# Attention stage: low halves of the weights by an adding DMA onto minus the high halves

## Chip, cores and metric

One core of a Trainium2 chip runs the whole kernel. The metric is the device time of one execution, in microseconds (us). All times are from runs on the chip.

## What is computed

A two-layer backbone over 512 latent tokens and 256 context tokens, model width 1024, everything in float32:

```python
for i in range(2):
    x = macaron_ffn(x, ...)                       # SwiGLU, width 2816
    xn = modulate(x, ...)                         # RMSNorm, scale and shift
    y = attn_mixer(xn, xn_ctx, ...) if i == 0 else conv_mixer(xn, ...)
    x = x + m[5] * y
    x = macaron_ffn(x, ...)
return rmsnorm(x, final_g)
```

The mixer of layer 0 is what matters here. One input projection gives queries, keys and values for 8 neighbourhood heads (an 8 x 16 window with a relative bias, plus all context keys) and for 4 differential heads (two softmax maps of each, the second subtracted with a factor lambda, then an RMSNorm). Their outputs are concatenated and go through one output projection.

## The kernel before

**Products.** TensorE multiplies in float32r, which keeps fewer bits than float32, so every operand is held as two float32r tiles, `hi` (rounded) and `lo` (what the rounding left). A float32 product is three of TensorE's: hi x hi, hi x lo and lo x hi (`mm3`, L134 to L140).

**Weights.** `load_w` (L109 to L116) brings one weight tile of 128x1024 float32 (512 KB) from HBM into a `raw` buffer by a DMA of SyncE's queue. ScalarE copies it to `hi`, which rounds (L114). Then one engine subtracts, `lo = raw - hi` (L115). `raw`, `wh` (hi) and `wl` (lo) have three buffers each, so a buffer comes free when the weight three before it has been used.

```python
nc.scalar.activation(hi[:, :n], raw[:, :n], AF.Copy)
(eng or wl_eng[0]).tensor_tensor(lo[:, :n], raw[:, :n], hi[:, :n], op=ALU.subtract)
```

**Who subtracts.** `wl_eng[0]` is VectorE for most of the kernel. For the attention stage it is set to GpSimd, because VectorE has the softmax there, and set back to VectorE after it. It is set after the first step of the projections, so that GpSimd subtracts for 23 weights: 13 of the query and key projections, 6 halves of value projections and 4 of the differential half of the output projection.

**Order of the stage.** Two generators run side by side. `projections()` emits the projections weight by weight. `attention()` emits, unit after unit, the scores, the softmax and the products with the values. A loop advances the projections by the time that the attention's products take on TensorE, so that TensorE has a projection to do while ScalarE and VectorE work at a softmax. A scheduler then puts each engine's instructions in an order of its own; every engine runs its own list strictly in that order.

Names that the prediction uses:
- L694: products of a value projection, L140 all others. L761 and L763: scores. L873 and L997: transposes of the weights of the softmax (`P`) before the products with the values, L888 and L973. L897: a product with ones, for the norm of a differential head; it waits for a square that ScalarE makes (L895).
- VectorE in the softmax of the differential heads: L846 the maximum, L853 to L855 small vectors, L856 to L858 scaling `P` and adding the second map. L248: a step of the head's norm. L754: the lo half of a key. L958: scaling `P` in the neighbourhood heads. L943 adds the bias.
- ScalarE: L848, L850, L851, L950 exponentials; L121 the hi half of what comes out of a product.
- GpSimd: L115 the 23 subtractions; L712 a product of the rotary embedding; L908 fills the bias tiles.

Of the kernel before, what the change touches and what calls it, by code (L numbers as in the profile page):

```python
# [10 lines left out]
F32R = mybir.dt.float32r  # L11
AF = mybir.ActivationFunctionType
ALU = mybir.AluOpType
# [5 lines left out]
KD = D // P            # chunks of the model width  # L19
N = 512                # latent tokens  # L20
NC = 256               # context tokens
# [7 lines left out]
BLOCKS = [(0, 4), (4, 4), (8, 4), (12, 6), (18, 4)]   # (first f chunk, chunks)  # L29
BLOCKS0 = [(0, 6), (6, 6), (12, 6), (18, 4)]                  # layer 0, first FFN  # L30
# [11 lines left out]
def build(tc, A, out):  # L42
    """A: name -> DRAM AP (host layouts, see kernel()); out: [128, 8, 512] feature-major."""
# [4 lines left out]
    with ExitStack() as es:  # L48
# [9 lines left out]
        def uid(s):  # L58
# [4 lines left out]
        BUFS = {"xn": 16, "h": 12, "P": 4,                                                 # 3 KB per partition  # L63
                "x": 12, "sc": 2, "pj": 6, "pv": 4, "P1": 4, "aux": 4,                     # 2 KB
                "nh": 7}                                                                   # 1 KB
# [7 lines left out]
        def tmp(n):  # L73
            """temporary of a norm"""
            if n > 256:
                return dt_("pj")
            return dp.tile([P, 256], F32, tag="nh", bufs=BUFS["nh"], name=uid("nh"))

# [16 lines left out]
        wl_eng = [nc.vector]  # L95

        def load_wx(src, tiles, lo):
            """in halves of 512 columns; tiles: two for each part"""
# [10 lines left out]
        def load_w(src, n=1024, eng=None):  # L109
            raw = wp.tile([P, 1024], F32, tag="raw", bufs=3, name=uid("raw"))  # L110
            nc.sync.dma_start(raw[:, :n], src)
            hi = wp.tile([P, 1024], F32R, tag="wh", bufs=3, name=uid("wh"))
            lo = wp.tile([P, 1024], F32R, tag="wl", bufs=3, name=uid("wl"))
            nc.scalar.activation(hi[:, :n], raw[:, :n], AF.Copy)  # L114
            (eng or wl_eng[0]).tensor_tensor(lo[:, :n], raw[:, :n], hi[:, :n], op=ALU.subtract)  # L115
            return hi, lo  # L116

        def split(hi, lo, src, scale=None):
            """hi + lo == src * scale exactly (scale a power of two)"""
# [9 lines left out]
        def after_mm(i):  # L129
            """not scheduled before the last matrix product emitted so far"""  # L130
# [4 lines left out]
        def mm3(outs, w, x, segs, first, last):  # L135
            """outs[i] += w^T x[:, segs[i]] with the three products that float32 needs"""
# [17 lines left out]
        wx = [dt_("x", dtype=F32R) for _ in range(4)]           # for weights of the start  # L154
# [4 lines left out]
        def load_c(nm):  # L159
            """silu of the vector on every partition"""  # L160
# [31 lines left out]
        def mod_step(l, m, ch, dve, pool=(), paced=True, early=False):  # L192
            """the streams in dve are summed on the vector engine, those in pool on GpSimd and ScalarE"""
# [38 lines left out]
        def mod_scale(l, m, i, s="c", out=None, ks=slice(0, KD)):  # L232
            """norm_g * (1 + scale)"""
# [6 lines left out]
        def rsqrt(ps, n, width):  # L240
            """(ps / width + eps) ** -0.5, with one Newton step after the table"""
# [10 lines left out]
        class Norm:  # L252
            """sum of squares gathered chunk by chunk (two partial sums), then 1/rms on every partition"""
# [5 lines left out]
            def add(self, xk, pre=False):  # L259
                """pre: have the table of rsqrt loaded by the time the sum is there"""  # L260
                n, i = self.n, min(self.k // 4, 1)
                if self.k >= self.parts:            # summed on the tensor engine
# [19 lines left out]
        def modulate_chunk(k, xk, y, s, b, hi, lo):  # L282
# [3 lines left out]
            if n <= 256 and k % 3 == 2:             # a part of them on ScalarE and GpSimd  # L286
# [12 lines left out]
        class Entry:  # L299
            """the input of a sub-layer: modulated norm of x, one token segment at a time"""  # L300
# [26 lines left out]
        class Head:  # L327
            """first products of a sub-layer, k outermost and one token segment at a time,
            so that they run while the rest of the input is still being made"""

            def __init__(self, units):
                # units: [(weight source, {segment: PSUM})], the PSUM allocated when used
# [3 lines left out]
            def run(self, e, si, ks=range(KD), inner=False):  # L336
                """inner: k innermost, so that the weights are freed one after the other"""
# [9 lines left out]
        def transition(e, down, head):  # L347
            """down(si): last products of the sub-layer before, segment si (calls e.norms[si].add);
            head(): makes the Head; statistics and products of neighbouring segments overlap"""
# [26 lines left out]
        def last_proj(e, srcs, nk, hl, evict):  # L376
            """output projection with nk chunks of input: the last three weight units are kept and used
            one token segment at a time"""
# [27 lines left out]
        class FFN:  # L406
# [6 lines left out]
            def head(self):  # L413
                """gate and up of chunk 0, gate of chunk 1"""
# [42 lines left out]
            def after_head(self, e):  # L457
                """finish chunk 1 (its up product); returns with chunks 0 and 1 done for the latents"""
# [31 lines left out]
            def body(self, e, first=2):  # L490
                """everything up to the last block's gate and up"""
# [10 lines left out]
            def tail(self, e2):  # L502
                """down products of the last block, one segment at a time"""
# [4 lines left out]
                held = {}                       # the three units loaded last  # L508
# [36 lines left out]
        # ================= layer 0: FFN 0 =================  # L545
        # the latents' part of the first chunks starts as soon as its modulation is there
# [83 lines left out]
        # ================= layer 0: attention =================  # L630
# [13 lines left out]
        # the residual waits in DRAM  # L644
# [4 lines left out]
        # differential lambda on every partition  # L649
# [22 lines left out]
        def proj_fm(src, outs):  # L672
            """outs: (segment, what takes the result) one after the other"""
# [9 lines left out]
        def proj_v(src, res, stack):  # L683
            """256 columns of a value projection, token-major, 3 tiles of 128 tokens per buffer: hi and lo in
            buffers of their own, or (stack) for each head of width 64 side by side, the second head lo first"""
# [30 lines left out]
        # Two heads (or maps) of width 64 share a chunk. For each, the moving operand stacks the  # L716
        # hi and lo parts of k over the 128 rows of the array and the stationary one holds hi of q
        # twice, so that one product gives qh kh + qh kl; ql kh is a second one on 64 rows.
# [3 lines left out]
        def q_parts(q, src, dst, scale):  # L722
            """src: 128 rows; dst: column view to write"""
# [32 lines left out]
        def scores(key, parts):  # L756
            """for (out, m, qs, ks) in parts: out = q k^T of head or map m, query columns qs, key columns given by
            the view ks; the products on 64 rows come together (outs in different banks)"""
# [64 lines left out]
        class Diff:  # L823
            """two query tiles of one differential head"""
# [77 lines left out]
        # neighbourhood heads: token order t' = column * 8 + row; query tiles are  # L902
# [359 lines left out]
```

## Time and profile before

| | |
|---|---|
| time, median of 3 runs | 2302.9 us |
| lowest, highest | 2297.8, 2303.41 us |
| span of the profiled execution | 2304.0 us |
| TensorE busy in that span | 2224.3 us, 97% |
| VectorE busy | 1372.8 us, 60% |
| ScalarE busy | 869.8 us, 38% |
| GpSimd busy | 284.1 us, 12% |
| mean granted TensorE clock | 0.989 |

The span runs from the first to the last instruction of one profiled execution; nothing else of that execution has a time of its own, and its span is 1.1 us over the median of the timed runs. A busy share is an average over stages. The stage that the change touches lies at about 655 to 985 us of the span.

### The profile page before, as it was taken

The numbers are of one execution on the slowest core, as the hardware profiler recorded it, in microseconds if no ns is written. First come the engines' busy times: TensorE is split into PE (matmuls) and PEld (weight loads), VectorE is DVE, ScalarE is ACT, GpSimd is POOL, SyncE is SP. The second block draws the span as 40 slices with busy tenths as digits, with TensorE's granted clock in tenths as the row PEclk, the third lists the DMA queues.
The fourth block names the chain that finished last, engine by engine and source line by source line (L and its number), as shares of the span: only waits on it lengthen the run. The fifth ranks groups of instructions, "written<-read, shape, count | busy, mean of one in ns | idle before, by whom it ended". The sixth has DMA issues, their size and how long they took to land.

```text
span 2304.0 us, 30465 instructions
## 1 busy us (share of the span) xinstructions
PE 2224.3 (97%) x11728; PEld 1889.3 (82%) x11728; DVE 1372.8 (60%) x2388; ACT 869.8 (38%) x1489; POOL 284.1 (12%) x196
## 2 busy tenths in 40 slices
PE   5899999999989999999999999999999999999998
PEld 3688888888878788788888888888889889888887
DVE  8893763534788876775555467555437446434335
ACT  4651421212456766652222244222225224222224
POOL 4550520000232311120000010000001001000001
PEclk9999999999999999999999999999999999999999
DMA  7672443434520111315555454444332322333232
GB/s 243 220 230 90 140 133 105 149 103 128 160 69 29 48 39 53 101 48 165 172 169 165 143 163 156 156 159 152 109 107 95 100 93 92 93 100 96 87 109 74
DMA packets 109993, 279.07 MB, mean 121 GB/s; under 512 B 14100, under 2 KB 18452, under 8 KB 109848
## 3 DMA queue, kind: packets, MB, share of 16 engines
q1 hardware_dynamic: 109848, 277.13, 38.5%
q8 instruction: 91, 1.49, 0.3%
q14 instruction: 54, 0.44, 0.1%
HBM read 272.88 MB, written 4.19 MB: 120 GB/s over the span
## 4 chain that ended last, share of the span: by engine, by line
PE 84%; DVE 10%; ACT 3%; issue 2%; POOL 1%; DMA 1%; SPq 0%; DVEq 0%; ACTq 0%; POOLq 0%
PE S L140 39%; PE acc L140 38%; PE acc L694 3%; DVE junk L210 1%; DVE wl L115 1%; PE S L763 1%; DVE xn L292 1%; PE acc L973 1%; DVE sm L215 1%; PE S L761 1%; PE acc L997 1%; DVE nh L285 1%; ACT wh L114 0%; POOL P L205 0%; PE acc L888 0%
## 5 line engine op out<-in xcount | busy, mean ns | idle before, releaser
L140 PE MATMUL S<-xn,wh 128*128 128x512 f32 (+1 forms) x3008 | 924.8, 380 | 20.8 <-ACT xn L291 12.5
L114 ACT ACTIVATE wh<-raw 128x1024 fp32r<-128x1024 f32 (+1 forms) x354 | 364.5, 1031 | 1072.2 <-PE acc L140 516.5
L140 PEld LDWEIGHTS S<-xn,wh 128*128 128x128 f32 x3008 | 555.9, 189 | 135.6 <-ACT xn L291 15.5
L115 DVE TENSOR_TENSOR wl<-raw,wh 128x1024 fp32r<-128x1024 f32 (+1 forms) x331 | 398.8, 1206 | 430.9 <-ACT wh L114 428.1
L140 PE MATMUL S<-xn,wl 128*128 128x512 f32 (+1 forms) x1504 | 569.0, 378 | 6.3 <-DVE wl L115 6.3
L140 PE MATMUL acc<-h,wh 128*128 128x512 f32 (+1 forms) x2148 | 534.6, 347 | 2.9 <-DVE x L470 2.8
L140 PE MATMUL acc<-xn,wh 128*128 128x256 f32 (+1 forms) x1664 | 451.1, 332 | 3.7 <-ACT xn L291 1.6
L140 PEld LDWEIGHTS acc<-h,wh 128*128 128x128 f32 x2148 | 364.2, 190 | 59.4 <-ACT h L121 3.1
L140 PE MATMUL acc<-h,wl 128*128 128x512 f32 (+1 forms) x1074 | 345.0, 344 | 1.4 <-DVE wl L115 1.4
L140 PEld LDWEIGHTS S<-xn,wl 128*128 128x128 f32 x1504 | 285.0, 190 | 61.5 <-DVE wl L115 8.3
L140 PEld LDWEIGHTS acc<-xn,wh 128*128 128x128 f32 x1664 | 297.1, 193 | 32.1 <-issue 2.7
L140 PE MATMUL acc<-xn,wl 128*128 128x256 f32 (+1 forms) x832 | 273.1, 329 | 3.2 <-DVE wl L115 3.2
L470 DVE SCALAR_TENSOR_TENSOR x<-acc,sm,x 128x512 f32<-128x512 f32 (+1 forms) x216 | 132.2, 629 | 220.1 <-PE acc L140 219.8
L140 PEld LDWEIGHTS acc<-h,wl 128*128 128x128 f32 x1074 | 192.4, 189 | 26.4 <-DVE wl L115 1.8
L270 POOL TENSOR_TENSOR nh<-nh,nh 128x256 f32<-128x256 f32 x42 | 45.4, 1085 | 1233.2 <-ACT nh L266 898.8
L210 DVE SCALAR_TENSOR_TENSOR junk<-aux,sc 128x512 bf16<-128x512 f32 x256 | 192.6, 752 | 1.6
L140 PEld LDWEIGHTS acc<-xn,wl 128*128 128x128 f32 x832 | 159.3, 192 | 16.9 <-DVE wl L115 4.1
L205 POOL TENSOR_TENSOR P<-aux,pv 128x512 f32<-128x512 f32 x64 | 106.3, 1674 | 131.5 <-ACT P L208 67.5
L121 ACT ACTIVATE h<-P 128x512 fp32r<-128x512 f32 (+2 forms) x99 | 62.5, 631 | 109.9 <-DVE P L429 109.8
L122 DVE TENSOR_TENSOR h<-P,h 128x512 fp32r<-128x512 f32 (+2 forms) x99 | 76.2, 769 | 20.1 <-ACT h L121 20.1
L694 PE MATMUL acc<-wh,xn 128*128 128x256 f32 x384 | 79.4, 295 | 1.5 <-DVE h L122 1.5
L115 POOL TENSOR_TENSOR wl<-raw,wh 128x1024 fp32r<-128x1024 f32 x23 | 56.7, 2468 | 185.6 <-ACT wh L114 185.6
(177 smaller groups left out, 1760.1 us busy)
## 6 DMA issues: line engine op xcount, KB each, us to landing
aux<-modw SPq DMA_DIRECT2D x288, 256.0 KB
raw<-wu SPq DMA_DIRECT2D x92, 512.0 KB
raw<-wg SPq DMA_DIRECT2D x91, 512.0 KB
raw<-wd SPq DMA_DIRECT2D x59, 512.0 KB
raw<-wd SPq DMA_DIRECT2D x48, 384.0 KB
raw<-cin SPq DMA_DIRECT2D x24, 512.0 KB
h<-modw SPq DMA_DIRECT2D x32, 256.0 KB
raw<-win SPq DMA_DIRECT2D x16, 512.0 KB
```

The costliest lines, as they stand in the source:

```text
L114: nc.scalar.activation(hi[:, :n], raw[:, :n], AF.Copy)
L115: (eng or wl_eng[0]).tensor_tensor(lo[:, :n], raw[:, :n], hi[:, :n], op=ALU.subtract)
L121: nc.scalar.activation(hi, src, AF.Copy)
L122: nc.vector.tensor_tensor(lo, src, hi, op=ALU.subtract)
L140: last_mm[0] = nc.tensor.matmul(o, a, b[:, s0:s1], start=first and ti == 0, stop=last and ti == 2)
L205: nc.gpsimd.tensor_mul(pr, raw, sc[s][h])
L210: i = nc.vector.scalar_tensor_tensor(junk, raw, 1.0, sc[s][h], op0=ALU.mult, op1=ALU.mult, accum_out=a)
L215: nc.vector.scalar_tensor_tensor(o[:, ch:ch + 1], pt[:, 0:1], pt[:, 1:2], modb[:, c:c + 1], op0=ALU.add, op1=ALU.add)
L270: (nc.gpsimd, nc.vector)[i].tensor_add(self.ss[i][:, :n], self.ss[i][:, :n], sq[:, :n])
L285: nc.vector.scalar_tensor_tensor(t[:, :n], xk, s[:, k:k + 1], y, op0=ALU.mult, op1=ALU.mult)
L470: nc.vector.scalar_tensor_tensor(v, ps, g[:, d:d + 1], v, op0=ALU.mult, op1=ALU.add)
L694: last_mm[0] = nc.tensor.matmul(o, a, b, start=k == 0 and ti == 0, stop=k == KD - 1 and ti == 2)
```

## The change

In the attention stage `lo` is made in another way. ScalarE writes minus the rounded weight into `lo`, a DMA issued from GpSimd's queue adds `raw` to it in place, and ScalarE then copies `raw` to `hi`. There is no subtraction on an engine there any more. Elsewhere nothing changes. The rest of the diff deletes comments and docstrings.

```diff
@@ load_w
             hi = wp.tile([P, 1024], F32R, tag="wh", bufs=3, name=uid("wh"))
             lo = wp.tile([P, 1024], F32R, tag="wl", bufs=3, name=uid("wl"))
+            if wl_eng[0] is None:
+                nc.scalar.activation(lo[:, :n], raw[:, :n], AF.Copy, scale=-1.0)
+                nc.gpsimd.dma_start(lo[:, :n], raw[:, :n], accum_op=ALU.add)
+                nc.scalar.activation(hi[:, :n], raw[:, :n], AF.Copy)
+                return hi, lo
             nc.scalar.activation(hi[:, :n], raw[:, :n], AF.Copy)
             (eng or wl_eng[0]).tensor_tensor(lo[:, :n], raw[:, :n], hi[:, :n], op=ALU.subtract)
@@ build, at the start of the attention stage
         advance()
-        wl_eng[0] = nc.gpsimd
+        wl_eng[0] = None
```

Lines of the changed kernel from L114 on: the two ScalarE copies are L115 (`lo`) and L117 (`hi`), the adding DMA is L116, and every line behind them stands 5 further down.

GpSimd's list at the start of the stage, before (`wl`, `wh` and `raw` are buffers of one weight each, `x` is of the rotary embedding):

```order
L115 TENSOR_TENSOR wl_6282<-raw_6279,wh_6281 128x1024
L115 TENSOR_TENSOR wl_6395<-raw_6392,wh_6394 128x1024
L115 TENSOR_TENSOR wl_6480<-raw_6477,wh_6479 128x1024
L115 TENSOR_TENSOR wl_6640<-raw_6637,wh_6639 128x1024
L712 TENSOR_TENSOR x_6379<-x_6379,x_5997 128x512
L115 TENSOR_TENSOR wl_6646<-raw_6643,wh_6645 128x1024
```

The same place now:

```order
L116 DMA wl_6282<-raw_6279 128x1024
L116 DMA wl_6396<-raw_6393 128x1024
L116 DMA wl_6482<-raw_6479 128x1024
L116 DMA wl_6643<-raw_6640 128x1024
L717 TENSOR_TENSOR x_6380<-x_6380,x_5997 128x512
L116 DMA wl_6650<-raw_6647 128x1024
```

Each subtraction has become the issue of a DMA at the same place of the list; the rotary products stand behind them as before.

ScalarE's list a little later, around the softmax of a differential head, before (`P` is the softmax of a unit, `S` its scores, `pv` the hi half of a transposed `P`):

```order
L121 ACTIVATE pv_6984<-acc_6979 128x512
L850 ACTIVATE P_6953,sm_6951<-S_6956,sm_6951 128x512
L851 ACTIVATE P_6954,sm_6951<-S_6956,sm_6951 128x256
L121 ACTIVATE pv_7005<-acc_7000 128x512
L114 ACTIVATE wh_7311<-raw_7309 128x1024
L848 ACTIVATE P_7032,sm_7031<-S_7035,sm_7031 128x768
L708 ACTIVATE x_7053<-acc_6975 128x512
```

The same place now:

```order
L126 ACTIVATE pv_6990<-acc_6985 128x512
L855 ACTIVATE P_6958,sm_6956<-S_6961,sm_6956 128x512
L856 ACTIVATE P_6959,sm_6956<-S_6961,sm_6956 128x256
L126 ACTIVATE pv_7011<-acc_7006 128x512
L117 ACTIVATE wh_7219<-raw_7217 128x1024
L117 ACTIVATE wh_7319<-raw_7317 128x1024
L853 ACTIVATE P_7038,sm_7037<-S_7041,sm_7037 128x768
L713 ACTIVATE x_7059<-acc_6981 128x512
L126 ACTIVATE pv_7088<-acc_7083 128x512
L855 ACTIVATE P_7039,sm_7037<-S_7042,sm_7037 128x512
L856 ACTIVATE P_7040,sm_7037<-S_7042,sm_7037 128x256
L115 ACTIVATE wl_7320<-raw_7317 128x1024
```

Ahead of the first exponential of the next softmax (L848 before, L853 now) there stood one copy of a weight, and now there are two; the second of these weights gets its `lo` only behind that softmax.

## Rows read from the trace of the kernel before

**Rows 1.** The page: shares of the chain that ended last, by engine.

```profile
PE 84%; DVE 10%; ACT 3%; issue 2%; POOL 1%; DMA 1%; SPq 0%; DVEq 0%; ACTq 0%; POOLq 0%
```

**Rows 2.** Stretch table of the stage: engines' busy us, then granted clock, DMA share, GB/s.

```profile
655.00:985.00 330.00, 307.01 (x1861) 260.10 (x1860) 253.24 (x448) 215.13 (x441) 69.92 (x34) 0.97 0.18 54
```

**Rows 3.** Page's costliest groups: GpSimd's subtractions (busy, mean ns, idle before).

```profile
L115 POOL TENSOR_TENSOR wl<-raw,wh 128x1024 fp32r<-128x1024 f32 x23 | 56.7, 2468 | 185.6 <-ACT wh L114 185.6
```

**Rows 4.** VectorE's instructions by line in the stage: ns min/median/max, first and last start.

```profile
L857 DVE SCALAR_TENSOR_TENSOR P<-P,sm,P x16: 736/744/2833, 682.0 to 827.8; 128x512 f32<-128x512 f32 x16
...
L858 DVE SCALAR_TENSOR_TENSOR P<-P,sm,P x16: 474/483/2602, 682.7 to 830.5; 128x256 f32<-128x256 f32 x16
...
L958 DVE TENSOR_SCALAR P<-P,sm x16: 475/486/2522, 846.8 to 974.4; 128x512 f32<-128x512 f32 x16
...
L754 DVE TENSOR_TENSOR h<-x,h x8: 684/686/2783, 661.4 to 779.0; 64x512 fp32r<-64x512 f32 x8
...
L248 DVE TENSOR_TENSOR nh<-nh,nh x8: 414/422/2450, 710.4 to 857.8; 128x256 f32<-128x256 f32 x8
...
L853 DVE TENSOR_TENSOR sm<-sm x16: 145/158/2348, 679.9 to 826.7; 128x1 f32<-128x1 f32 x16
```

**Rows 5.** Timeline at 682 us: start, us, engine, instruction, [idle before it].

```profile
682.25 5.31 POOL L115 TENSOR_TENSOR wl<-raw,wh 128x1024 fp32r<-128x1024 f32 x2 [17.23 <-ACT wh L114]
...
682.70 2.60 DVE L858 SCALAR_TENSOR_TENSOR P<-P,sm,P 128x256 f32<-128x256 f32 x1
```

**Rows 6.** Chain that ended last, in the stage: start, us, what.

```profile
662.79 2.78 DVE h L754
...
682.78 2.52 DVE P L858
685.30 2.28 DVE sm L853
...
763.29 1.06 ACT wh L114
...
827.79 2.83 DVE P L857
...
859.06 1.06 ACT wh L114
...
938.25 2.52 DVE P L958
```

**Rows 7.** Timeline of TensorE: products before which it idled.

```profile
667.13 0.39 PE L694 MATMUL acc<-wh,xn 128*128 128x256 f32 x1 [1.46 <-DVE h L122]
...
728.18 0.70 PE L897 MATMUL acc<-nh,ones 128*128 128x256 f32 x2 [2.79 <-ACT nh L895]
...
772.37 0.70 PE L897 MATMUL acc<-nh,ones 128*128 128x256 f32 x2 [1.31 <-ACT nh L895]
...
941.26 0.55 PE L761 MATMUL S<-h,pj 128*128 128x256 f32 x1 [2.63 <-DVE S L943]
```

**Rows 8.** Stretch table: one of 20 us (columns as in rows 2).

```profile
680.00:700.00 20.00, 17.18 (x85) 13.26 (x85) 17.24 (x30) 10.71 (x22) 7.99 (x4) 0.91 0.19 56
```

**Rows 9.** ScalarE's copies of weights in the stage: ns min/median/max, first and last start.

```profile
L114 ACT ACTIVATE wh<-raw x26: 1053/1060/1075, 661.4 to 982.2; 128x1024 fp32r<-128x1024 f32 x26
```

**Rows 10.** Timeline: two weights' copies on ScalarE, their first hi x lo products on TensorE.

```profile
749.15 1.06 ACT L114 ACTIVATE wh<-raw 128x1024 fp32r<-128x1024 f32 x1 [1.11 <-PE acc L694]
...
763.74 0.39 PE L140 MATMUL acc<-xn,wl 128*128 128x512 f32 x1
...
908.69 1.06 ACT L114 ACTIVATE wh<-raw 128x1024 fp32r<-128x1024 f32 x1 [0.88 <-PE acc L694]
...
922.47 0.40 PE L140 MATMUL acc<-xn,wl 128*128 128x512 f32 x1
```

**Rows 11.** One weight load: its issue, and DMA busy tenths, 699 to 704 in 40 slices.

```profile
699.75 0.35 SPq L111 DMA_DIRECT2D raw<-win  x1
...
DMA  0000000000000996994368999897323021000000
```

## The prediction

> **What bounds the kernel now.** The chain of work that ended last says that TensorE is the bound: 84% of it, VectorE 10%, ScalarE 3% [rows 1]. So a change beside TensorE counts only where TensorE waits for it. The stretch table of the stage says how much that is: of 330 us TensorE is busy 307.0, so 23.0 us are idle, and the granted clock is 0.97, so part of it ran at 1.2 GHz in place of 2.4. VectorE is busy for 253.2 us, ScalarE for 215.1, GpSimd for 69.9 [rows 2]. The 23 subtractions make 56.7 us of GpSimd's time, and behind GpSimd nobody waits for them in that row or in the chain [rows 1, 3]. Read that far, the change looks like work moved off an idle engine.
>
> The groups by line say otherwise. The same VectorE instruction takes 0.48 us as a rule and up to 2.60 (L858), 0.16 and up to 2.35 (L853, one number per partition), 0.49 and up to 2.52 (L958) [rows 4]. The timeline shows why: the 2.60 us of L858 begin at 682.70, after GpSimd has begun two subtractions at 682.25 [rows 5]. A VectorE instruction that comes up during a subtraction ends only when the subtraction does, and a subtraction takes 2.47 us [rows 3]. And these are not idle instructions: nine stretched ones, of 2.28 to 2.83 us, stand in the chain of the stage, the first at 662.79, the last at 938.25 [rows 6].
>
> **What the removal of the subtractions gives.** The nine pieces (one each of L754, L853, L248 and L958, two of L857, three of L858) add up to 22.9 us. At their lines' medians [rows 4] they would take 0.69 + 3 x 0.48 + 0.16 + 0.42 + 2 x 0.74 + 0.49 = 4.7 us. The difference is 18.2 us.
>
> From below I bound it by TensorE's idle time. Six idle times stand behind stretched instructions, the first 1.46 us at 667.13, the last 2.63 at 941.26, 14.5 us in all. Two of them, as the 2.79 at 728.18, are before L897, where TensorE idles for 1.31 us without any subtraction too [rows 7], so 14.5 - 2 x 1.31 = 11.9 us are the subtractions' own. From above there is the clock. In the 20 us after one such wait it reads 0.91 [rows 8]: 0.09 x 20 = 1.8 us lost at the lower level. Over the whole stage the loss is 0.03 x 330 = 9.9 us [rows 2]; the one dip at the start of the stage, behind a wait for VectorE's own last subtractions, stays, so 8.1 may come back. Ends: 11.9 and 20.0 us. I take 18.2, the chain's own figure, which lies near the upper end because a shorter wait also spares the low clock.
>
> **What ScalarE pays.** 23 more copies at 1.06 us [rows 9], 24.4 us on an engine that is busy for 65% of the stage. In the chain three of the 23 copies appear, the first at 763.29, the last at 859.06, 1.06 us each [rows 6]: 3.2 us if each is followed by a second one. The order of the changed program does that at the first of them: two copies stand ahead of the next softmax's first exponential where one stood. With VectorE's stretches gone ScalarE is later relative to it, so I count as many again: 6.4 us. Ends: 3.2 and 24.4.
>
> **What the DMA costs.** Nothing, as long as it lands before the first product with `lo`. Nothing in this trace adds by DMA, so I bound it. A load of the same 512 KB was issued at 699.75; its bytes run from 700.6 to 702.9, 3.2 us after the issue [rows 11]: the lower end, 1.0 us to start and 2.3 of moving. For the upper end I let three passes of the bytes (read `raw`, read `lo`, write `lo`) follow one another, 6.9 us, put one whole load of 2.3 ahead of them, and give GpSimd as long for the issue as for a subtraction: 1.0 + 6.9 + 2.3 + 2.5 = 12.7 us. I take 8, in the middle, since DMA engines stand at a share of 0.18 in the stage [rows 2] and no load is likely to be ahead.
>
> The cover: the tightest weight's copy begins at 908.69 and ends 1.06 later, and its first product with `lo` begins at 922.47, 12.7 us later; the next one has 763.74 - 750.21 = 13.5 [rows 10]. The others have more. Eight fits; 12.7 just does. Where the `lo` copy has moved behind a softmax, as in the order of the change, part of the cover goes with it; for the two tightest weights the changed program makes `lo` first, so I count none of it lost. If the cover goes, TensorE waits for the rest of the DMA, weight by weight.
>
> **What else moves.** `raw` is now held until the DMA has landed and `hi` is made, a few us longer than before; the load that waits for it on SyncE's queue, and the bias tiles' loads behind that, are late by as much. Of the 330 us a weight takes 14 on average and three buffers are loaded ahead, so I cost it at nothing. On GpSimd the rotary products (L712) stand behind the issues instead of behind 2.5 us subtractions: nothing, or a gain. No weight product is added or removed.
>
> **Sum.** 2304.0 - 18.2 + 6.4 = 2292.2 us for the profiled execution; the median of the runs is 1.1 us under that span, so I forecast **2291 us**, 12 less. Ends of the terms: 2302.9 - 20.0 + 3.2 = 2286 and, with the low gain and half of ScalarE's upper end, 2302.9 - 11.9 + 12.2 = 2303. A measurement of this kernel tells a difference from 0.3% on, that is, outside 2296 to 2310.
>
> **Rivals.**
>
> *ScalarE takes the gain back.* If half of the new copies or more fall ahead of something that TensorE waits for, they cost 12.2 us and up. For it: ScalarE at 65% and in strict order, with softmax and evictions in one list. Against: three in 23 were on the chain. With the 18.2 gained, 2302.9 - 18.2 + 12.2 = 2297; with all 24.4, 2309. Its middle is 2302: no change.
>
> *The adding DMA is late: slower.* It decides from the point where the two tightest weights alone eat the gain: (L - 12.7) + (L - 13.5) = 11.8, so at L = 19 us from copy to landing; earlier, if others join. At L = 25 these two cost 12.3 + 11.5 = 23.8, which gives 2291 + 24 = **2315**, and more with each further weight. For it: three buffers, a DMA that reads two streams and writes one, and a queue that no instruction of this kernel has used for data. Against: even my upper end is 12.7. The Trainium skill, "DMA: Bandwidth & Descriptors", section "Anatomy of one DMA", fits a DMA from GpSimd's queue as 2.0 us + bytes / 436 GB/s, an estimate of 3.2 us for 512 KB, or 4.4 with the second stream counted as bytes; it is fitted to plain copies and no run here shows it. By it this rival would hardly have a chance; by the rows it keeps 0.15.
>
> *GpSimd still holds VectorE up.* The issue on GpSimd may stretch VectorE as a subtraction did; then the change does not do what it says. L958, which has one tile from SBUF and a scalar, was stretched just as those with two [rows 4]. If all issues hold as long as subtractions, nothing is gained and 6.4 lost: 2309. The Trainium skill, "SBUF — State Buffer", section "Who interferes with whom", has the second input of a two-input VectorE instruction shut out only by a GpSimd instruction that reads SBUF, and has descriptor writing need the write side alone. By that L857, L858, L853, L754 and L248 would run free and only L958's kind could be held, which would leave the sum at 2291 + 2 = 2293; the trace shows the blocking of both kinds, and no issue of this sort.
>
> **Chances.** Forecast 0.58, ScalarE's rival 0.18, late DMA 0.15, GpSimd's hold 0.09. Faster by over 0.3%: 0.58 and a little of the last, 0.60. Within 0.3%: most of ScalarE's rival and half of the last, 0.20. Slower: the late DMA and the far ends of the other two, 0.20. The range reaches from the best ends of both terms, 2286, less 6 of the 23.0 - 14.5 = 8.5 us that TensorE idles for other reasons and that a changed order of its products may spare, 2280, to just past the first price of the late DMA, 2316; beyond it I leave a little under one in ten, and as much below.
>
> **What would show it.** Right: L857, L858, L248, L853 and L958 at their medians with no 2.5 us maximum; GpSimd's busy time in the stage down by 57 us; TensorE's idle time in the stage down from 23 to 12 or so and its clock near 0.99; ScalarE 24 us busier; no TensorE wait that ends with the adding DMA. Wrong: TensorE waiting before a product with `wl` for a DMA; stretched VectorE instructions under the issues; or more idle time before L897 and the transposes, ended by ScalarE behind two copies.

## The result, and the profile after

The changed kernel takes **2278.11 us** (median of four runs, 2277.15 to 2284.59), the kernel before 2303.15 (2297.8 to 2308.35, four runs): a ratio of **0.9906, 95% interval 0.9884 to 0.9928**. A second set of both, later, gave 2283.08 against 2301.95, a ratio of 0.9920 (0.9893 to 0.9947). So the change is a gain, of 25 us in the first set and 19 in the second. The forecast was 2291, a gain of 12, in a range of 2280 to 2316: the first median lies 1.9 us under the lower end of that range, the second inside it.

The page of the changed kernel, first part (busy time by engine) and fourth (the chain that ended last):

```profile
PE 2210.0 (97%) x11728; PEld 1880.5 (83%) x11728; DVE 1350.6 (59%) x2388; ACT 890.5 (39%) x1512; POOL 244.0 (11%) x196
...
PE 85%; DVE 8%; ACT 3%; issue 2%; DMA 1%; POOL 1%; SPq 0%; DVEq 0%; ACTq 0%; POOLq 0%
```

VectorE's share of the chain fell from 10% to 8% [rows 1], ScalarE's stayed.

To see where the time went I compare stretches that begin and end at the same product: the stage from the 3,200th to the 4,000th product of line 140 (145 in the changed kernel). The stretch table gives, behind the length, the busy time of PE, PEld, DVE, ACT and POOL, then the granted clock, the DMA share and GB/s. What is left of the length after PE's busy time is TensorE's idle time; products at the low clock show as more busy time. The first row is a piece of the FFN ahead of the stage. The kernel before, its first and its second trace:

```profile
300.00:360.00 60.00, 60.00 (x342) 51.99 (x341) 30.98 (x59) 15.56 (x30) 6.11 (x4) 1.00 0.40 119
621.40:978.70 357.30, 334.41 (x2101) 288.70 (x2099) 280.19 (x505) 232.55 (x483) 83.40 (x44) 0.97 0.20 59
```

```profile
300.00:360.00 60.00, 60.00 (x342) 52.04 (x341) 31.06 (x61) 15.56 (x30) 7.46 (x5) 1.00 0.38 121
623.10:979.10 356.00, 333.95 (x2101) 288.53 (x2099) 280.22 (x505) 232.44 (x483) 83.31 (x44) 0.97 0.19 60
```

The changed kernel, its first and its second trace:

```profile
300.00:360.00 60.00, 60.00 (x349) 52.48 (x348) 30.85 (x60) 15.35 (x30) 6.82 (x4) 1.00 0.37 119
613.90:951.90 338.00, 327.89 (x2101) 283.86 (x2099) 258.46 (x506) 253.13 (x507) 46.76 (x44) 0.99 0.39 99
```

```profile
300.00:360.00 60.00, 60.00 (x342) 52.05 (x341) 30.82 (x59) 14.97 (x30) 6.59 (x4) 1.00 0.38 119
620.00:958.00 338.00, 327.90 (x2101) 284.01 (x2099) 258.56 (x505) 253.10 (x506) 46.79 (x44) 0.99 0.39 99
```

Two things stand there. **The stage** is 19.3 us shorter (357.3 to 338.0; 18.0 by the second traces). Idle time makes 12.8 of it (22.9 to 10.1), busy time 6.5 (334.4 to 327.9, for the same 2,101 products): less of it at the low clock, 0.97 to 0.99. **The FFN ahead of it**, which the change does not touch, runs at one of two paces: 342 or 349 products in 60 us, at clock 1.00 and without a gap in both. The pace is worth 6.6 us over that FFN (from the 1,000th product to the 3,000th 345.8 us or 352.4). The first trace of the changed kernel had the faster pace, its second the slower, so the change does not settle it. Whether it makes the faster one likelier stays open: the two traces of the kernel before and the two experiments without the copy of minus `raw` (the first two below) all have the slower one, and of the ten traces with that copy six have the faster.

So of the 27.2 us between the first two profiled spans (2304.0 and 2276.8) 19.3 are the stage, 6.6 the pace and 1.3 the rest. The second traces, both at the slower pace, differ by 19.0 (2306.3 and 2287.3). The rest is not exact to a few us: outside the stage these four traces and the second of the changed kernel, all at the slower pace, take between 1944.7 and 1950.3 us. In the stage, where it acts, the change is worth **18 to 19 us**.

The groups of the changed kernel that answer to [rows 4] (duration in ns, least, median, most):

```profile
L863 DVE SCALAR_TENSOR_TENSOR P<-P,sm,P x16: 473/478/486, 674.4 to 810.2; 128x256 f32<-128x256 f32 x16
...
L862 DVE SCALAR_TENSOR_TENSOR P<-P,sm,P x16: 735/742/754, 673.7 to 809.6; 128x512 f32<-128x512 f32 x16
...
L963 DVE TENSOR_SCALAR P<-P,sm x16: 474/486/489, 822.0 to 947.5; 128x512 f32<-128x512 f32 x16
...
L858 DVE TENSOR_TENSOR sm<-sm x16: 146/154/163, 671.5 to 808.4; 128x1 f32<-128x1 f32 x16
```

No maximum of these groups is off its median any more, and the same holds for the lo half of a key and the step of the norm (L754 and L248 before). The timeline at one of the new issues: VectorE's L862 begins 0.09 us after GpSimd's issue and takes its 0.74 us. VectorE, then GpSimd:

```profile
765.21 0.74 DVE L862 SCALAR_TENSOR_TENSOR P<-P,sm,P 128x512 f32<-128x512 f32 x1
...
765.12 0.88 POOL L116 DMA_DIRECT2D wl<-raw  x1 [6.93 <-ACT wl L115]
```

VectorE began 42 instructions inside a subtraction in the stage of the kernel before, and 11 of them were stretched; in the changed kernel it began 30 inside an issue, and none was. The other 31 show who is not held: 25 of them read a tile of PSUM (`acc`, `S`), six a single tile of SBUF (`x`, `sm`). This maximum over scores took its usual 0.96 us with a subtraction running all the time (kernel before, GpSimd, then VectorE):

```profile
697.33 2.40 POOL L115 TENSOR_TENSOR wl<-raw,wh 128x1024 fp32r<-128x1024 f32 x1 [9.76 <-ACT wh L114]
...
697.61 0.96 DVE L846 TENSOR_REDUCE sm<-S 128x1 f32<-128x768 f32 x1 [1.84 <-PE S L763]
```

And the adding DMA's line in the changed kernel, where nobody stands under the heading of those who waited:

```profile
L116 POOL DMA_DIRECT2D wl<-raw x23: 852/859/1007, 655.3 to 927.7; - x23
...
who waited for it (us, times):
...
DMA to landing us min/median/max: 4.5/4.8/6.6
```

### The profile page after: what moved, and what is told of

Same layout as the page of the kernel before. It is cut to its first block, busy times and chain, and to the rows that moved or that the text cites. A ratio compares the mean times of both kernels' runs of the same rounds, so it can differ in the third digit from the quotient of the medians.

```text
span 2276.8 us, 30529 instructions
## 1 busy us (share of the span) xinstructions
PE 2210.0 (97%) x11728; PEld 1880.5 (83%) x11728; DVE 1350.6 (59%) x2388; ACT 890.5 (39%) x1512; POOL 244.0 (11%) x196
## 4 chain that ended last, share of the span: by engine, by line
PE 85%; DVE 8%; ACT 3%; issue 2%; DMA 1%; POOL 1%; SPq 0%; DVEq 0%; ACTq 0%; POOLq 0%
PE S L145 39%; PE acc L145 38%; PE acc L699 3%; DVE junk L215 1%; DVE wl L120 1%; PE S L768 1%; DVE xn L297 1%; PE S L766 1%; DVE sm L220 1%; DVE nh L290 1%; PE acc L978 1%; PE acc L893 1%; PE acc L1002 1%; POOL P L210 0%; PE acc L878 0%
## 5 line engine op out<-in xcount | busy, mean ns | idle before, releaser
L145 PE MATMUL S<-xn,wh 128*128 128x512 f32 (+1 forms) x3008 | 919.9, 379 | 20.7 <-ACT xn L296 12.7
L119 ACT ACTIVATE wh<-raw 128x1024 fp32r<-128x1024 f32 (+1 forms) x331 | 340.3, 1029 | 1049.9 <-PE acc L145 509.5
L434 DVE TENSOR_TENSOR P<-P,S 128x512 f32<-128x512 f32 (+1 forms) x91 | 59.8, 657 | 10.4 <-ACT P L433 9.6
```

What stands on the lines that cost most here:

```text
L145: last_mm[0] = nc.tensor.matmul(o, a, b[:, s0:s1], start=first and ti == 0, stop=last and ti == 2)
L434: nc.vector.tensor_mul(sl[:, s0:s1], sl[:, s0:s1], uu)
```

## The experiments

Theory C: the gain is the end of GpSimd's hold on VectorE, less a small price for ScalarE's copies (S). Rival O: the gain comes from the other order of TensorE's products that the change brings. Open beside them: how large each part is, whether a late DMA was near, and the pace.

### The subtractions on VectorE

```diff
-        wl_eng[0] = nc.gpsimd
+        wl_eng[0] = nc.vector
```

> The kernel before with the stage's 23 subtractions on VectorE (1.2 us each, 28 us more on an engine busy for 253 of 330 us), GpSimd left with its rotary products and the bias tiles. Theory C (what the change gave is the end of GpSimd's hold on VectorE): the stretched pieces of 2.3 to 2.8 us are gone from the chain (-18 us) and VectorE's 28 us come back in part, a third of them on the chain: 2303 - 18 + 9 = 2294, with VectorE's groups at their medians. Rival O (the gain came from another order of TensorE's products, the hold cost little): VectorE only gets more to do, 2303 + 9 or more = 2312.

Measured 2285.25 us, ratio to the kernel before 0.9941 (0.9916 to 0.9966). The stage:

```profile
621.10:965.80 344.70, 332.75 (x2101) 287.21 (x2099) 284.31 (x528) 233.33 (x483) 26.23 (x21) 0.98 0.20 62
```

It is 12.6 us shorter than before though VectorE has more to do, and L857, L858, L754 and L958 are at their medians. That speaks for C: taking the work off GpSimd pays even where it is put onto the engine that was held up. TensorE's order is a little different here too, so this run alone does not shut out rival O.

### No copy of minus `raw`

```diff
-                nc.scalar.activation(lo[:, :n], raw[:, :n], AF.Copy, scale=-1.0)
-                nc.gpsimd.dma_start(lo[:, :n], raw[:, :n], accum_op=ALU.add)
+                pass
+                nc.gpsimd.dma_start(lo[:, :n], raw[:, :n])
```

> The changed kernel without the copy of -raw: the DMA writes raw into lo without adding (the low half is then the weight itself and not the remainder). ScalarE has 23 copies as before, GpSimd has the issues, and the order of the instructions on TensorE and VectorE is that of the kernel before. Theory C with S: the end of the hold alone, without ScalarE's price: 2278 - 6 = 2272, so 31 us under the kernel before. Rival O (order): with the order of before the time goes back towards it, 2290 or more. Rival with ScalarE's copies free: 2278.

Measured 2278.75 us, 0.9894 (0.9864 to 0.9924). The stage, and the DMA's line:

```profile
621.10:956.20 335.10, 327.13 (x2100) 283.88 (x2099) 258.44 (x505) 232.31 (x483) 39.61 (x44) 0.99 0.31 99
```

```profile
L116 POOL DMA_DIRECT2D wl<-raw x23: 527/527/848, 660.4 to 930.2; - x23
...
DMA to landing us min/median/max: 2.9/3.1/6.3
```

TensorE, VectorE and ScalarE run the list of the kernel before here, instruction for instruction, and the stage is 22.2 us shorter than before: rival O falls. This is the hold alone: idle time 22.9 to 8.0, so 14.9 us, and busy time 334.4 to 327.1, so 7.3. From here to the changed kernel the stage grows by 2.9 us (335.1 to 338.0), 2.1 of it idle time. That is the price of ScalarE's 23 copies (with the addition and the changed order in it, which this run does not tell apart). The medians cannot show it: 2278.75 lies 0.6 above the changed kernel's first median and 4.3 below its second.

### GpSimd's hold put back, in halves and whole

```diff
                 nc.scalar.activation(hi[:, :n], raw[:, :n], AF.Copy)
-                return hi, lo
+                [nc.gpsimd.tensor_tensor(junk, raw[:, z:z + N], hi[:, z:z + N], op=ALU.subtract) for z in (0, N)]; return hi, lo
```

> The changed kernel, and behind each weight's copies GpSimd subtracts raw - hi once more, in two halves, into a scratch tile that nobody reads; the order of the instructions on TensorE, VectorE and ScalarE is that of the changed kernel. Theory C: the hold is back, stretched VectorE pieces of 1.3 to 2.8 us stand in the chain again, and 18 to 20 us are lost: 2278 + 19 = 2297, clock in the stage back to about 0.97. Rival O (order): 2278, since the order is untouched. Rival D (only GpSimd's own lateness counted): the DMA issues behind the subtractions come 2.5 us later, cover 12.7: 2278.

```diff
                 nc.scalar.activation(hi[:, :n], raw[:, :n], AF.Copy)
-                return hi, lo
+                nc.gpsimd.tensor_tensor(junk[:, :n], raw[:, :n], hi[:, :n], op=ALU.subtract, saturate=False); return hi, lo
...
-        junk = const.tile([P, N], mybir.dt.bfloat16, name="junk")
+        junk = const.tile([P, 2 * N], mybir.dt.float8e4, name="junk")
...
```

> The changed kernel, and behind each weight's copies one whole subtraction raw - hi on GpSimd into a scratch tile nobody reads (1 KB a partition, the scratch of the modulation sums, here of one byte an element); order on TensorE, VectorE and ScalarE as in the changed kernel. Against the run with halves this doubles the length of one hold (2.4 us in place of 1.3) at the same total. Theory C (a hold costs by its length, because VectorE waits for the end of the instruction that it met): stretched VectorE pieces up to 2.8 us, 15 to 22 us lost in the stage, 2278 + 18 = 2296, twice the price of the halves (9). Rival (the price follows GpSimd's busy time, not the length of a piece): 2287, as with halves. Rival O: 2278.

Halves: 2287.45 us, 0.9941 (0.9916 to 0.9967). Whole: 2294.16 us, 0.9970 (0.9952 to 0.9989). The stage and GpSimd's group with halves:

```profile
614.40:959.30 344.90, 332.63 (x2101) 287.33 (x2099) 265.92 (x505) 253.47 (x506) 108.93 (x90) 0.98 0.38 97
```

```profile
L118 POOL TENSOR_TENSOR junk<-raw,wh 128x512 bf16<-128x512 f32 x46 | 63.1, 1371 | 46.9 <-issue 28.5 <-ACT wh L117 16.5
```

and whole, with a piece of VectorE's timeline and of GpSimd's:

```profile
611.30:963.40 352.10, 334.64 (x2100) 286.95 (x2099) 274.91 (x505) 253.93 (x506) 102.57 (x67) 0.98 0.38 95
```

```profile
L118 POOL TENSOR_TENSOR junk<-raw,wh 128x1024 fp8e4<-128x1024 f32 x23 | 56.7, 2466 | 49.9 <-ACT wh L117 22.8 <-PE acc L1002 12.1 <-PE acc L902 5.8
```

```profile
745.74 2.90 DVE L862 SCALAR_TENSOR_TENSOR P<-P,sm,P 128x512 f32<-128x512 f32 x1
748.57 2.70 DVE L863 SCALAR_TENSOR_TENSOR P<-P,sm,P 128x256 f32<-128x256 f32 x1
...
745.71 2.39 POOL L118 TENSOR_TENSOR junk<-raw,wh 128x1024 fp8e4<-128x1024 f32 x1 [4.66 <-ACT wh L117]
748.58 2.40 POOL L118 TENSOR_TENSOR junk<-raw,wh 128x1024 fp8e4<-128x1024 f32 x1 [0.49 <-POOL junk L118]
```

The order on the three other engines is that of the changed kernel in both. Halves cost the stage 6.9 us (344.9 against 338.0), whole pieces 14.1 (352.1), at 63.1 and 56.7 us of GpSimd's time. So not GpSimd's busy time is paid for but the length of one piece, as C said. That the price just doubles is not shown: with halves 8 VectorE instructions were stretched, by 7.3 us together, with whole pieces 6, by 9.9, and the whole pieces write into a scratch of another type. L862 takes 2.90 us beside a subtraction and 0.74 beside an issue. Of the 22.2 us that the hold cost in the order of before, it costs 14.1 in the order of the changed kernel, where it met fewer: 11 instructions were stretched before, by 21.0 us together.

### One copy more on ScalarE

```diff
                 nc.scalar.activation(hi[:, :n], raw[:, :n], AF.Copy)
-                return hi, lo
+                [nc.scalar.activation(junk, raw[:, z:z + N], AF.Copy) for z in (0, N)]; return hi, lo
```

> The changed kernel with a third copy of each weight on ScalarE, in two halves into a scratch tile that nobody reads: about 23 x 1.2 = 28 us more on ScalarE. Theory S (a copy on ScalarE costs about a quarter to 0.4 of its length, as the prediction took: 6.4 us for the 24.4 of the change): 2278 + 7 to 11 = 2285 to 2289, with more idle time of TensorE ended by ScalarE. Rival: ScalarE's copies are wholly beside the chain, then 2278 and the 6.4 us of the prediction were nothing; or ScalarE is at its limit, then 2278 + 20 = 2298.

Measured 2291.74 us, 0.9956 (0.9939 to 0.9972). The stage and the new group:

```profile
619.10:969.20 350.10, 334.13 (x2100) 286.34 (x2099) 260.51 (x505) 277.88 (x552) 46.68 (x44) 0.98 0.38 95
```

```profile
L118 ACT ACTIVATE junk<-raw 128x512 bf16<-128x512 f32 x46 | 28.9, 629 | 12.1 <-DMA raw<-wv 7.0 <-DMA raw<-win 4.6
```

The stage grows by 12.1 us for 28.9 of ScalarE's time, just above the 7 to 11 of S, where the change's own 24.3 us cost 2.9. The price of a copy is not one number. Why these cost more is not shown: ScalarE also stood for 11.6 us before them until a load of `raw` had landed, which it never did in the stage of the changed kernel, and the list on TensorE and VectorE differs a little from the changed kernel's.

### The two copies exchanged

```diff
+                nc.scalar.activation(hi[:, :n], raw[:, :n], AF.Copy)
                 nc.scalar.activation(lo[:, :n], raw[:, :n], AF.Copy, scale=-1.0)
                 nc.gpsimd.dma_start(lo[:, :n], raw[:, :n], accum_op=ALU.add)
-                nc.scalar.activation(hi[:, :n], raw[:, :n], AF.Copy)
```

> The changed kernel with the two copies of ScalarE exchanged: hi first, then minus hi and the adding DMA. Order on TensorE and VectorE as in the changed kernel; hi is there 1.06 us earlier, lo lands 1.06 us later, some 7 us after hi's copy where 12.7 are covered. Theory S (what ScalarE's new copies still cost, 2 to 3 us of TensorE's idle time, is hi being late by one copy): the stage's idle time falls from 10.1 to about 8, so 2 us less at the same pace of the FFN before. Rival (it is everything queued behind the pair of copies that is late, softmax and norm, which the exchange doesn't help): 10.1 again, no change.

Measured 2284.14 us, 0.9913 (0.9886 to 0.9941). The FFN's piece and the stage:

```profile
300.00:360.00 60.00, 60.00 (x341) 52.08 (x340) 31.02 (x59) 15.55 (x30) 6.10 (x4) 1.00 0.38 118
620.90:958.70 337.80, 327.72 (x2101) 283.70 (x2099) 258.55 (x506) 253.25 (x507) 46.72 (x44) 0.99 0.39 99
```

10.1 us of idle time again, in the same places: the rival's number came out. `hi` was not what came late, and `lo` could land a copy later for nothing. That it is the softmax and the norm behind the copies is likely and not shown. The trace is at the slower pace (341 products).

### A late DMA

```diff
-                nc.gpsimd.dma_start(lo[:, :n], raw[:, :n], accum_op=ALU.add)
+                [nc.gpsimd.dma_start(lo[:, :n], raw[:, :n], accum_op=ALU.add) for _ in range(4)]
```

> The changed kernel with the addition done four times, one DMA after the other (each waits for the one before to land), so lo is four times raw minus the high half and not the remainder; four issues on GpSimd a weight, whose queue waits in between. From copy to landing 1.06 + 4 x 4.8 = 20 us instead of 6. The prediction's price for a late DMA: the two tightest weights have 12.7 and 13.5 us of cover, so 7.3 + 6.5 = 14 us: 2278 + 14 = 2292, with TensorE waiting for the DMA before products with wl. Rival (cover is larger than the rows of before say, or the order of the changed list makes room): 2278 to 2283. Rival (GpSimd's waits also hold up the rotary products): more than 2300.

Measured 2382.69 us, 1.0357 (1.0330 to 1.0384), with the stage

```profile
613.60:1052.40 438.80, 362.32 (x2101) 308.12 (x2099) 260.47 (x505) 253.90 (x506) 106.19 (x113) 0.88 0.74 159
```

and this of the DMA's line:

```profile
L116 POOL DMA_DIRECT2D wl<-raw x92: 850/859/1212, 655.0 to 1041.6; - x92
...
who waited for it (us, times):
  POOL wl L116: 248.0, 68
...
  PE acc L145: 38.9, 9
...
  PE acc L699: 21.0, 5
DMA to landing us min/median/max: 4.5/5.4/9.6
```

The stage is 100.8 us longer. The first two numbers were far off; "more than 2300" came out, but not for its reason, since no wait of TensorE names the rotary products. The run did not test lateness but rate. In the changed kernel the 23 issues lie (927.7 - 655.3) / 22 = 12.4 us apart; four additions, one behind the other with GpSimd's queue waiting, take longer than that (92 issues in 386.6 us, about 17 a weight), so the weights fell behind. What it does show is how a late DMA looks: TensorE's products wait for it by name, 14 times for 59.9 us, and the clock falls to 0.88. In the changed kernel no wait ends so. From which lateness a single weight begins to cost stays open.

### The switch to the adding DMA earlier, and kept longer

Two weights earlier:

```diff
+        wl_eng[0] = None
         advance()
-        wl_eng[0] = None
```

> The changed kernel with the switch to the adding DMA two weights earlier, ahead of the stage's first projection. In the changed kernel TensorE idles for 3.64 us at 648.58 until VectorE's last wl, and the clock is at 0.5 for 6.8 us from 650.82 on (3.4 us lost). Theory I (the stage's length is a fixed amount of product time, plus TensorE's idle time, plus what the low clock loses, so that an idle time that goes takes its dip along): both go, less 1 to 2 us for another wait: 5 us less in that place, 2278 - 5 = 2273. Rival (the two weights are late by any road, as their loads come last): the wait ends with the adding DMA or ScalarE instead, 2278 or up to 2281.

Ahead of the transition:

```diff
+        wl_eng[0] = None
         transition(e, f0.tail(e), head0)
...
-        wl_eng[0] = None
```

> The changed kernel with the switch still earlier, ahead of the last products of the FFN before, so that all weights of the transition are made by adding DMA. VectorE loses about ten subtractions of 1.3 us where it is busy for 51 of 55 us, ScalarE (35 of 55) gets ten copies of 1.06. Theory I: as in the run with two weights, and VectorE's norm work comes earlier: 2278 - 7 = 2271. Rival (ScalarE's table and norm work of the transition is the chain): the copies stand ahead of it, 2278 or up to 2284.

Two weights earlier as in the first, and kept to the end of the next transition:

```diff
+        wl_eng[0] = None
         advance()
-        wl_eng[0] = None
...
-        wl_eng[0] = nc.vector
...
-        transition(e, down, f1.head)
+        transition(e, down, f1.head); wl_eng[0] = nc.vector
```

> The run with two weights more, and the adding DMA kept for the output projection and the first weights of the next FFN. In the changed kernel TensorE idles there for 1.01, 1.41 and 1.71 us from 974.60 to 990.78, the second until VectorE's wl, with a dip of 6.8 us at 988.7. Theory I: the 1.41 and perhaps half of the dip's 3.4 us go: 2273 - 3 = 2270. Rival: the dip stays with the other two waits (norm on VectorE, xn on GpSimd): 2273 - 1.

Measured 2290.6 us (0.9950, 0.9932 to 0.9968), 2295.46 (0.9970, 0.9953 to 0.9987) and 2288.43 (0.9945, 0.9924 to 0.9966): none beats the changed kernel, and the three stages are 6.6, 7.6 and 7.7 us longer than its 338.0 (the third holds 2,106 products). The stage of the first, and TensorE's timeline where the 3.64 us had been:

```profile
614.70:959.30 344.60, 333.00 (x2101) 287.09 (x2099) 256.69 (x503) 255.35 (x508) 47.16 (x46) 0.98 0.40 100
```

```profile
656.11 0.80 PE L766 MATMUL S<-h,pj 128*128 128x512 f32 x1 [5.14 <-DVE h L759]
```

The stage of the second, and its longest wait by group:

```profile
624.20:969.80 345.60, 329.77 (x2101) 284.87 (x2099) 251.41 (x499) 258.57 (x512) 48.54 (x50) 0.99 0.45 110
```

```profile
L145 PE MATMUL acc<-h,wl 128*128 128x256 f32 x23 | 7.7, 337 | 3.7 <-DMA wl<-raw 3.7
```

Theory I fails in all three, and each cost more than its rival allowed. In the first the wait for VectorE's `wl` is gone and a longer one, for VectorE's parts of k, stands there; a second stretch at the low clock comes with it, shown in the last section. In the second the adding DMA is late, in a transition whose loads come close together: there the cover of the stage does not exist. The third gained nothing behind the stage either: from its end to the program's end 1326.8 us, 1324.9 in the changed kernel.

### Both kernels once more

> The kernel before once more, unchanged, for its trace. The profiles so far run the layer-0 FFN (from 240 us on) at one of two paces: 349 products in 60 us (the changed kernel) or 342 (the kernel before), TensorE fully busy at clock 1.00 in both. Theory P (the pace is a state of the execution, whatever the kernel): either pace may come; with 349 the span is 2304 - 7 = 2297, with 342 about 2304. Rival (the change brings the faster pace): always 342 here.

> The changed kernel once more, unchanged. Theory P: either pace; with 349 a span of 2277, with 342 one of 2284. In the stage as before: idle time of TensorE 10 us and one dip of the clock, at its start. Rival (the stage's clock differs from execution to execution too): more dips, 1.7 or 3.4 us each.

Measured 2301.54 us for the kernel before (0.9997, 0.9980 to 1.0014, against its own other runs), and 2283.08 for the changed one (0.9920). Their rows stand above: the changed kernel came at the slower pace, and its stage was the same to 0.1 us. Theory P holds for the changed kernel, which showed both paces; the kernel before showed the slower one twice, which leaves its rival standing for that kernel. The stage is the place of the gain again.

## Why the prediction was right, and where it was off

**Direction and mechanism: right.** TensorE is the bound, what the 23 subtractions cost lay in VectorE's stretched pieces, and with them gone TensorE waits less. The runs with the hold put back, and the run with the order of before, show it. One sentence was too wide: not every VectorE instruction that comes up during a subtraction ends only with it. 31 of 42 took their usual time, L846 above with 2.1 us of the subtraction to go. The pieces that the prediction counted were stretched ones, so its sum does not suffer.

**The step that failed is the size of the relief.** The prediction said: "I take 18.2, the chain's own figure, which lies near the upper end because a shorter wait also spares the low clock." It took the clock to be inside the chain's 18.2. It is not: the chain's stretched pieces are VectorE's time; what the low clock costs shows as longer products, in TensorE's own share. Measured without ScalarE's copies, the relief is 14.9 us of idle time and 7.3 of busy time, 22.2 together, above the end of 20.0. The clock's part was well bounded (8.1); the idle part was bounded at 11.9 from the six waits behind stretched pieces, less 2 x 1.31 for what TensorE would wait before L897 in any case [rows 7], and came out 3 larger. The waits before that line (902 in the two others) show most of it; the kernel before, the run without the copy of minus `raw`, and the changed kernel (us, times):

```profile
  ACT nh L895: 9.4, 5
```

```profile
  ACT nh L900: 1.7, 2
```

```profile
  ACT nh L900: 3.1, 4
```

These waits name ScalarE, but with the holds gone most of them go. What stays is this, in the run without the copy:

```profile
720.00 0.48 PE L902 MATMUL acc<-nh,ones 128*128 128x256 f32 x1 [0.68 <-ACT nh L900]
...
760.87 0.48 PE L902 MATMUL acc<-nh,ones 128*128 128x256 f32 x1 [1.04 <-ACT nh L900]
```

The second is the 1.31 us at 772.37 of before, with no subtraction beside it: it was there in any case, as the prediction said. But it does not stand for the two waits from which it was taken off: of the 2.79 us at 728.18 the 0.68 of the first line stays, and of the other, 3.54 at 833.94, nothing. So 0.68 had to be taken off and not 2.62, which is 1.9 of the 3 us; a wait of 1.27 us at 791.79, left out of the six, went as well.

**ScalarE's term was too large**: 6.4 us taken, 3.2 as the lower end, 2.9 measured. "I count as many again" had no row behind it. Both errors lean the same way, 4.0 and 3.5 us, which makes 19.3 of 11.8. The rest of the first set's 25 us fits the draw of the pace, which no row of one trace could tell. The terms' own best end was 2286, above both medians; that the range reached to 2280 is owed to 6 us for a changed order of TensorE's products, and the order is not where the gain came from: there it was luck.

**The idle time came out as written** ("from 23 to 12 or so and its clock near 0.99"; 10.1 and 0.99): the forecast's net 11.8 was near the idle time's 12.8, and the clock's 6.5 came on top. That is partly luck, as the 11.8 was a sum of two terms that were both off.

**The DMA: right at nothing.** From the copy's begin to landing it is 5.8 to 8.1 us in the two traces of the changed kernel, at most about the 8 taken and far under 12.7, so this rival deserved less than its 0.15 in the stage. In a place with less cover it came true: the run with the switch ahead of the transition. The Trainium skill, "DMA: Bandwidth & Descriptors", section "Anatomy of one DMA", was near: the estimate from its fit was 3.2 us for the plain copy, where the trace has 3.1 from issue to landing, and 4.4 for the adding one with the second stream counted, where it has 4.8.

**GpSimd's hold by the issue: none that was met.** Of the two-input L862 and L863 five began inside an issue, and none was stretched. No L963 met an issue in either trace of the changed kernel, so for L958's kind the question stays nearly open: in the run without the copy one L861, which also has one tile and a scalar, began 0.11 us after an issue of 0.85 us and took its usual 0.61. The 2 us set aside for that kind were not needed. What the Trainium skill, "SBUF — State Buffer", section "Who interferes with whom", says of VectorE instructions with two inputs from SBUF, that a GpSimd instruction which reads SBUF holds them and one that only writes there does not, agrees with the 2.90 us of L862 beside a subtraction, and with its 0.74 beside an issue if an issue only writes there, which no run shows.

**GpSimd's busy time fell by 36.6 us in the stage, not 57**: the issues take 0.86 us each, 19.9 in all, which the list of signs had left out. It costs nothing here, as none of those that were met held VectorE.

ScalarE became 20.6 us busier, not 24 (232.55 to 253.13).

**ScalarE takes the gain back: not here.** But the run with one more copy lost 12.1 us; the rival was one copy away.

## What to carry to other kernels

A wait that goes gives back two terms on TensorE: the idle time, which the chain and the idle rows show, and the low clock behind it, which shows as busy time; add them, and read both from one stretch that begins and ends at the same product. GpSimd's subtractions beside VectorE were paid for by the length of their single pieces and not by GpSimd's share, so look at the maxima of VectorE's groups before calling GpSimd idle, and at which of VectorE's instructions are stretched: here those that read `acc` or `S` were not. Before a difference of 0.3% between two traces is put down to a change, look whether a stretch that the change does not touch differs too, and take a second trace of each.

## What the runs showed of the hardware that was not expected

**A stretch of products has two paces.** The FFN of layer 0, same instructions, clock 1.00, no gaps: 342 products in 60 us or 349. It stays for the whole FFN and differs between two executions of the changed kernel. What sets it stays open.

**The same wait is followed by a low clock in one kernel and not in another.** Before the same product the run with the switch two weights earlier and the changed kernel idle for 0.77 and 0.76 us:

```profile
717.37 0.80 PE L902 MATMUL acc<-nh,ones 128*128 128x256 f32 x1 [0.77 <-ACT nh L900]
```

```profile
714.17 0.48 PE L902 MATMUL acc<-nh,ones 128*128 128x256 f32 x1 [0.76 <-ACT nh L900]
```

and the stretch behind it is at 1.2 GHz (0.50) in the one, with 20 products, and at 2.4 GHz (1.00) in the other, with 42:

```profile
716.80:723.60 6.80, 6.23 (x20) 4.48 (x20) 3.36 (x9) 6.06 (x12) 0.00 (x0) 0.50 0.66 154
```

```profile
713.60:720.40 6.80, 6.23 (x42) 5.28 (x43) 6.00 (x13) 6.06 (x12) 0.00 (x0) 1.00 0.63 154
```

Just ahead of it both idled alike (0.49 and 0.44 us before two products of L893 in the first, 0.48 and 0.45 in the second). At the stage's start the first had waited 5.14 us and the second 3.64; what decides was not tried. So a term for the clock is to be given with both ends.

**Adding makes a DMA dearer on both sides**: 0.86 us of GpSimd's time to issue against 0.53 for the plain copy of the same 512 KB, and 4.8 us to land against 3.1.
